# Splitting weights by two software DMAs instead of by engine subtraction, in a two-layer RWKV / attention / convolution network

## The chip, the cores and the metric

One core of a Trainium2 chip runs the whole program. The metric is device time in microseconds (us) of one execution, as the median of three runs. Engines are TensorE (PE; PEld is its weight load), VectorE (DVE), ScalarE (ACT), GpSimd (POOL) and SyncE (SP); 16 DMA engines move data.

## The reference, cut to what matters

```python
def reference(x, ...):                       # x: 1 x 1024 x 1024, float32
    for layer in range(2):
        h = rmsnorm(x, norm_mix_g[layer])
        if layer == 0:
            mix = hybrid_mixer(h, ...)       # h @ w_in, rwkv scan + window attention, @ w_out
        else:
            mix = conformer_conv(h, ...)     # h @ pw1, gate, 31-tap convolution, norm, silu, @ pw2
        x = x + mix
        h = rmsnorm(x, norm_ffn_g[layer])
        x = x + jnp.square(jax.nn.relu(h @ w1[layer])) @ w2[layer]   # 1024 -> 4096 -> 1024
    return rmsnorm(x, final_norm_g)
```

All is float32. Each of the large products (w_in, w_out, pw1, pw2, w1, w2) multiplies a weight matrix with 1024 tokens.

## The kernel before

Tokens are taken in two halves of 512; features lie on the 128 partitions. TensorE multiplies the 32-bit type fp32r, which is narrower than float32. So each operand is split into a high part (the value rounded to fp32r) and a low part (the value minus the high part), and each product is three matmuls that add up in PSUM (`mm3`, lines 299 to 301): high times high, high weights times low activations, low weights times high activations. One `mm3` is one block of 128 x 128 weights by 512 tokens.

Weights are read again for each half of the tokens. `weights` (line 273) brings them: a column block is cut into two tiles of 128 x 512 elements (256 KB), called halves below. The tile of w_in, w_out, pw1, pw2 and w1 takes four 128 x 128 blocks, in runs of 512 B in DRAM; that of w2 takes 2 x 256 columns, in runs of 1 KB. There are 720 halves: 80 of w_in, 32 of w_out, 96 of pw1 and pw2, 512 of the MLPs. For each half

- SyncE's queue loads the raw values into `wraw` (line 284),
- ScalarE casts them to fp32r in `whi` (line 286),
- VectorE or GpSimd writes `wlo = wraw - whi` (lines 288 and 271). `dve` chooses: two of three calls go to VectorE where it is None; w_in goes to VectorE where it is True; `mlp` of the stages that run beside a convolution is called with False, so there all subtractions, those of the hidden layer too (`hidl`), are on GpSimd.

`wraw`, `whi` and `wlo` have four slots each, taken in turn (`Ring`, line 1365), so a tile waits until TensorE is done with the half four before it.

The program has these stages. `run` first weaves (`weave`) the input projection, eight rwkv scans, the attention, w_out of the first half and the MLP of layer 0 for the first half into one order by hand on TensorE; this lasts about 1000 us and is called the mixer here. Then follow w_out of the second half, `conv_in(0)`, the MLP of layer 0 on the second half while VectorE does the first convolution (`conv`, line 1226: 30 multiply-adds of 128 x 512 for each of 8 channel blocks), `conv_norm`, `conv_out`, `conv_in(1)`, the MLP of layer 1 on the first half beside the second convolution, and the rest of that MLP with the last norm. Apart from the mixer on TensorE, a scheduler at build time sets the order on every engine; each engine and each DMA queue then runs its instructions strictly in that order.

Other work that the steps name: line 385 (`first_back`) reads the stored first norm `hd` back with eight transfers on GpSimd's queue; line 1183 adds an MLP product into `x`; line 1457 copies the tail of a convolution input on GpSimd; lines 617, 654 and 508 are small GpSimd steps of the scans (`BD`, `E`) and of the token shift (`carry`); lines 1157, 1158 and 1162 are relu, square and cast of the hidden layer on ScalarE.

Of the kernel before, what the change touches and what calls it, by code (L numbers as in the profile page):

```python
# [9 lines left out]
F32 = mybir.dt.float32  # L10
F32R = mybir.dt.float32r
AF = mybir.ActivationFunctionType
ALU = mybir.AluOpType
AX = mybir.AxisListType
PSUM = bass.MemoryType.PSUM
DRAM = bass.MemoryType.DRAM

P = 128
# [15 lines left out]
class Ring:  # L34
    """slots taken in turn, from one or several pools"""
# [10 lines left out]
class Net:  # L46
# [25 lines left out]
    # ---------------------------------------------------------------- order on the tensor engine  # L72
    def go(self, gen):
        """a stream on its own"""
        while True:
            try:
                next(gen)
            except StopIteration as e:
                return e.value

    def weave(self, base, *gens):
        """several streams in one order: the first of gens that is due goes on, base between them, so that the array
        stays busy; a stream yields the time (us) that its next products have to wait for the other engines, or the
        name of what has to be there"""
        due = [[0.0, g] for g in gens]
        rest = [[0.0, base]]
        share = 0.0

        def first(ds):
            return next((d for d in ds if (d[0] in self.done if isinstance(d[0], str) else d[0] <= self.clk)), None)  # L90

        while due or rest:
            f, b = first(due), first(rest)
            d = f if f and (share < LAG["SHARE"] or not b) else b
            if d is None:
                self.clk = min(d[0] for d in due + rest if not isinstance(d[0], str))
                continue
            t = self.clk
            try:
                w = next(d[1])  # L100
                d[0] = w if isinstance(w, str) else self.clk + w + (LAG["SLACK"] if w else 0.0)
            except StopIteration:
                (due if d is f else rest).remove(d)
            t = self.clk - t
            share = share + t if d is f else max(0.0, share - LAG["RATIO"] * t)

    # ---------------------------------------------------------------- constants
# [62 lines left out]
    def warm(self):  # L170
        """products that nobody reads, while the array would only wait: so its clock stays up for the first columns"""
        ps = self.mmps()
        for _ in range(4):
            self.nc.tensor.matmul(ps[:, 0:256], lhsT=self.ones, rhs=self.rst[:, 0:256], start=True, stop=True)
# [89 lines left out]
    # ---------------------------------------------------------------- helpers  # L264
    def lo(self, out, x, hi, dve=None):
        """out = x - hi, for the second part of an operand"""
        if dve is None:
            self.nlo += 1
            dve = self.nlo % 3 != 0
        eng = self.nc.vector if dve else self.nc.gpsimd  # L270
        eng.tensor_tensor(out=out, in0=x, in1=hi.bitcast(F32), op=ALU.subtract)  # L271

    def weights(self, aps, a, b, dve=None):
        """blocks of weights in two parts, k by k; loaded and split one half of them after the other"""
# [6 lines left out]
        for i in range(2):  # L281
            for ap, (his, los) in zip(aps, ws):
                raw = self.wraw.tile([P, h, b], F32, "wraw")
                nc.sync.dma_start(out=raw, in_=ap[:, i * h:(i + 1) * h, :])
                hi = self.whi.tile([P, h, b], F32R, "whi")
                nc.scalar.copy(out=hi, in_=raw)  # L286
                lo = self.wlo.tile([P, h, b], F32R, "wlo")
                self.lo(lo, raw, hi, dve)
# [33 lines left out]
    def norm_first(self, hf, rows, dst):  # L322
        """first rmsnorm by rows, then turned to feature-major; dst(u, g): where the two parts go"""
# [42 lines left out]
    def first_stored(self):  # L366
        """the second half's first norm, kept in DRAM until its place is free"""
# [20 lines left out]
    def colsum(self, xs, sq, k="n"):  # L388
        """sum over channels of x (or of its square), in two parts"""
# [29 lines left out]
    def rstd(self, accs, eps, pool, k="n"):  # L419
        """1 / sqrt(mean + eps) for every token, on every partition"""  # L420
# [56 lines left out]
    # ---------------------------------------------------------------- input projection  # L477
# [10 lines left out]
    def w_in_pair(self, js, hs):  # L488
        """two columns side by side, channel block by channel block: what is there first is used first"""
# [31 lines left out]
    # ---------------------------------------------------------------- rwkv  # L521
    def scan(self, hf, p, r, k, v, la, gl, sset, ptag, ahead):
# [86 lines left out]
        # unit lower triangular inverse: 16-blocks by substitution, then two merges  # L609
# [97 lines left out]
        # per chunk: state' = M state + C, output = R state + Y  # L707
# [114 lines left out]
    # ---------------------------------------------------------------- attention  # L822
    def attention(self, hf, i, z, qs, mi):
        """query heads 2i and 2i+1"""
# [54 lines left out]
    # ---------------------------------------------------------------- mixer of one half  # L879
# [14 lines left out]
    def shift(self, hf, j, ps, keep=False, hp=False):  # L894
        """one 128-channel column of the input projection of the rwkv part, shifted"""
# [18 lines left out]
    def twice(self, j, rows, cols, width):  # L914
        """64 channels of a column, on both halves of the partitions; cols: (from, of which half's column) pieces"""
# [6 lines left out]
    def att_in(self, hf):  # L922
        """keys with one block of the half before in front: the high part of each kv head on both halves of the
        partitions, the low parts of the first on the upper one and of the second on the lower one; values by rows"""
# [23 lines left out]
    def queries(self, hf, i, z):  # L948
        """two heads' queries, each with its high part on the half of the partitions where the low part of its keys is
        and its low part on the other one"""  # L950
# [10 lines left out]
    def att(self, hf, z):  # L961
        """attention of one half: query heads 4z to 4z+3"""
# [26 lines left out]
    def cols0(self, hs):  # L989
        """the first half's input projection"""  # L990
# [23 lines left out]
    def last1(self, h1):  # L1014
        """the last two columns, under the norm"""
# [20 lines left out]
    def scans(self, z, todo):  # L1036
        """scans one after the other in one set of tiles"""
# [39 lines left out]
    def w_out(self, hf, mi, xs, w_):  # L1077
        """output projection; the second half's input is there, the first half's comes along;
        the first half's first two columns begin with what is done, while the last scan and the attention go on"""
# [56 lines left out]
    # ---------------------------------------------------------------- mlp  # L1136
    def mlp(self, layer, halves, blocks, ahead, dve=None, close=None):
        """halves: list of (x tiles, (hi, lo)); blocks of 512 hidden channels;
        ahead: how many 128-channel pieces of a block go before the second product of the block in front;
        close: takes the second product of the last block"""  # L1140
# [57 lines left out]
    # ---------------------------------------------------------------- convolution  # L1198
# [66 lines left out]
    def row_rstd(self, ss, n):  # L1265
        """1 / sqrt(mean + eps) from n sums of squares of every row"""
# [10 lines left out]
    def final(self, hf, xs):  # L1277
        """last rmsnorm, by rows again"""
# [19 lines left out]
    def final_rows(self, hf, xs, w2, his, los):  # L1298
        """what is there so far by rows, and the second product of the last block by rows; then the last rmsnorm, one
        block of tokens after the other"""  # L1300
# [50 lines left out]
    # ---------------------------------------------------------------- the whole  # L1351
# [152 lines left out]
```

## Time and profile before

| | |
|---|---|
| median of 3 runs | 2522.08 us (2516.49, 2522.08, 2525.11) |
| span of the profiled execution | 2519.2 us, 2.9 below the median; no other time is listed for it |
| TensorE, VectorE, ScalarE, GpSimd busy | 93%, 62%, 42%, 33% |
| chain that ended last, by engine | TensorE 64%, VectorE 28%, ScalarE 3%, DMA 3% |
| mean granted TensorE clock | 0.968 |
| DMA | 236.19 MB, mean 94 GB/s; SyncE's queue 30.2% of 16 engines' span, GpSimd's 0.6% |

Busy shares are averages over stages with different limits, so they say which engines can be a bound, not where. The windows by stage and the waits say the latter. Matmuls are pipelined: one takes 389 ns in the rows, but they start 0.227 us apart, so a half (12 of them) takes 2.72 us.

### The profile page before, as it was taken

How to read it: one execution, taken by the hardware profiler on the slowest of the kernel's cores; microseconds unless marked ns; L12 is line 12 of the kernel's file. 1: busy time of each engine (PE TensorE's matmuls, PEld its weight loads, DVE VectorE, ACT ScalarE, POOL GpSimd, SP SyncE). 2: the span in 40 equal slices, each digit the busy share in tenths (PEclk: the TensorE clock that was granted, in tenths of full speed). 3: DMA queues.
4: the chain of work that ended last, by engine and by line, in shares of the span. 5: the costliest groups of instructions: out<-in, count | busy, mean ns of one | idle time of the engine just before them, and what ended most of it. 6: DMA issues, size and time to landing. Idle time of an engine off the chain costs nothing.

```text
span 2519.2 us, 38162 instructions
## 1 busy us (share of the span) xinstructions
PE 2355.4 (93%) x14525; PEld 1875.1 (74%) x14525; DVE 1568.6 (62%) x2613; ACT 1055.3 (42%) x1888; POOL 843.9 (33%) x676
## 2 busy tenths in 40 slices
PE   7999899899999999999678999997779999999998
PEld 6776677767777778777566888876657888888887
DVE  6766745647573646499998403899998025533333
ACT  6546645445352424344223543523225434433333
POOL 2223333111111112126547664226456643212221
PEclk9999999989999999999898999999889999999999
DMA  6435324313122223323112333332222332433332
GB/s 210 115 108 147 93 67 147 101 58 90 56 70 85 74 81 101 101 84 101 59 59 76 101 98 99 93 88 84 67 67 80 101 100 88 127 100 96 97 99 85
DMA packets 371851, 236.19 MB, mean 94 GB/s; under 512 B 39522, under 2 KB 355156, under 8 KB 371668
## 3 DMA queue, kind: packets, MB, share of 16 engines
q1 hardware_dynamic: 367604, 225.89, 30.2%
q0 software_dynamic: 2176, 4.19, 0.6%
q10 hardware_dynamic: 1888, 3.67, 0.4%
q8 instruction: 114, 1.87, 0.3%
q14 instruction: 69, 0.57, 0.1%
HBM read 215.35 MB, written 18.35 MB: 93 GB/s over the span
## 4 chain that ended last, share of the span: by engine, by line
PE 64%; DVE 28%; ACT 3%; DMA 3%; issue 2%; SPq 0%; POOL 0%; ACTq 0%; DVEq 0%; POOLq 0%
PE mm L299 19%; PE mm L300 18%; PE mm L301 18%; DVE acc L1226 17%; DVE x L1183 1%; DVE wlo L271 1%; DVE nt L472 1%; PE sc L603 1%; DMA raw<-p 1%; PE sc L685 1%; DVE E L662 1%; DVE C L660 1%; DVE h L271 1%; PE sc L768 1%; PE at L842 1%
## 5 line engine op out<-in xcount | busy, mean ns | idle before, releaser
L271 POOL TENSOR_TENSOR wlo<-wraw,whi 128x512 fp32r<-128x512 f32 x448 | 630.6, 1411 | 1293.6 <-ACT whi L286 1223.3
L286 ACT CAST whi<-wraw 128x512 fp32r<-128x512 f32 x720 | 445.1, 620 | 1065.8 <-PE mm L300 911.0
L299 PE MATMUL mm<-h,whi 128*128 128x512 f32 x1792 | 730.3, 408 | 10.7 <-DVE x L1183 7.1
L301 PE MATMUL mm<-h,wlo 128*128 128x512 f32 x1792 | 707.2, 395 | 7.5 <-DVE wlo L271 7.5
L300 PE MATMUL mm<-h,whi 128*128 128x512 f32 x1792 | 706.4, 394 | 0.5 <-DVE h L271 0.3
L299 PE MATMUL mm<-hidh,whi 128*128 128x512 f32 x992 | 396.0, 401 | 77.0 <-DVE x L1183 75.4
L1226 DVE SCALAR_TENSOR_TENSOR acc<-u,par,acc 128x512 f32<-128x512 f32 x480 | 466.7, 1030 | 0.1
L299 PEld LDWEIGHTS mm<-h,whi 128*128 128x128 f32 x1792 | 340.5, 190 | 93.6 <-issue 18.1
L301 PEld LDWEIGHTS mm<-h,wlo 128*128 128x128 f32 x1792 | 340.4, 190 | 85.3 <-DVE wlo L271 11.6
L301 PE MATMUL mm<-hidh,wlo 128*128 128x512 f32 x992 | 389.8, 395 | 11.2 <-POOL wlo L271 11.2
L300 PEld LDWEIGHTS mm<-h,whi 128*128 128x128 f32 x1792 | 341.3, 190 | 67.8 <-issue 2.0
L300 PE MATMUL mm<-hidl,whi 128*128 128x512 f32 x992 | 390.0, 394 | 0.3 <-DVE hidl L271 0.2
L1183 DVE TENSOR_TENSOR x<-mm,x 128x512 f32<-128x512 f32 x248 | 167.6, 685 | 291.9 <-PE mm L301 291.7
L271 DVE TENSOR_TENSOR wlo<-wraw,whi 128x512 fp32r<-128x512 f32 x272 | 194.6, 717 | 202.7 <-ACT whi L286 194.4
L299 PEld LDWEIGHTS mm<-hidh,whi 128*128 128x128 f32 x992 | 189.3, 191 | 123.1 <-issue 80.7
L301 PEld LDWEIGHTS mm<-hidh,wlo 128*128 128x128 f32 x992 | 189.1, 191 | 52.2 <-POOL wlo L271 11.6
L300 PEld LDWEIGHTS mm<-hidl,whi 128*128 128x128 f32 x992 | 189.6, 191 | 39.8 <-issue 1.1
L271 POOL TENSOR_TENSOR hidl<-rel,hidh 128x512 fp32r<-128x512 f32 x77 | 113.1, 1468 | 44.3 <-ACT hidh L1162 25.1
L1158 ACT ACTIVATE rel<-rel 128x512 f32<-128x512 f32 x128 | 80.6, 632 | 3.5
L1157 ACT ACTIVATE rel<-mm 128x512 f32<-128x512 f32 x128 | 75.5, 592 | 5.9 <-DVE u L1217 4.8
L1164 DVE CAST hidh<-rel 128x512 fp32r<-128x512 f32 x68 | 31.4, 464 | 52.5 <-ACT rel L1158 52.4
L473 ACT CAST h<-nt 128x512 fp32r<-128x512 f32 x48 | 29.7, 621 | 56.9 <-DVE nt L472 56.5
(357 smaller groups left out, 2257.3 us busy)
## 6 DMA issues: line engine op xcount, KB each, us to landing
wraw<-in_mlp_w_dram SPq DMA_DIRECT2D x512, 256.0 KB
wraw<-in_cv_pw_w_dram SPq DMA_DIRECT2D x96, 256.0 KB
wraw<-in_hy_w_in_dram SPq DMA_DIRECT2D x80, 256.0 KB
wraw<-in_hy_w_out_dram SPq DMA_DIRECT2D x32, 256.0 KB
p<-stg SPq DMA_DIRECT2D x30, 256.0 KB
raw<-p SPq DMA_DIRECT2D x40, 128.0 KB
krv<-p SPq DMA_DIRECT2D x18, 256.0 KB
xrow<-in_x_dram SPq DMA_DIRECT2D x8, 512.0 KB
```

The costliest lines, as they stand in the source:

```text
L271: eng.tensor_tensor(out=out, in0=x, in1=hi.bitcast(F32), op=ALU.subtract)
L286: nc.scalar.copy(out=hi, in_=raw)
L299: mm(ps, lhsT=whi, rhs=xhi, start=start, stop=False)
L300: mm(ps, lhsT=whi, rhs=xlo, start=False, stop=False)
L301: mm(ps, lhsT=wlo, rhs=xhi, start=False, stop=stop)
L472: nc.vector.scalar_tensor_tensor(out=t, in0=xs[c], scalar=self.pv(gname, c), in1=r, op0=ALU.mult, op1=ALU.mult)
L473: nc.scalar.copy(out=his[c], in_=t)
L1157: nc.scalar.activation(out=t, in_=ps, func=AF.Relu)
L1158: nc.scalar.activation(out=t, in_=t, func=AF.Square)
L1164: nc.vector.tensor_copy(out=hi, in_=t)
L1183: nc.vector.tensor_tensor(out=x, in0=pss[o], in1=x, op=ALU.add)
L1226: nc.vector.scalar_tensor_tensor(out=acc, in0=u[:, j:j + H], scalar=self.pv(f"dw{j}", c), in1=acc, op0=ALU.mult, op1=ALU.add)
```

## The change

Only `weights` changes in what it does; everything else in the diff takes out comments and docstrings. The raw tile goes away. A transfer on GpSimd's queue casts the weights from DRAM into `whi`; ScalarE writes `-whi` into `wlo`; a second transfer on GpSimd's queue reads the same weights again and adds them onto `wlo`. `dve` no longer plays a part for weights; `self.nlo`, which counts calls to share the other subtractions, is still counted up.

```diff
         ws = [([], []) for _ in aps]
         for i in range(2):
             for ap, (his, los) in zip(aps, ws):
-                raw = self.wraw.tile([P, h, b], F32, "wraw")
-                nc.sync.dma_start(out=raw, in_=ap[:, i * h:(i + 1) * h, :])
+                src = ap[:, i * h:(i + 1) * h, :]
                 hi = self.whi.tile([P, h, b], F32R, "whi")
-                nc.scalar.copy(out=hi, in_=raw)
+                nc.gpsimd.dma_start(out=hi, in_=src)
                 lo = self.wlo.tile([P, h, b], F32R, "wlo")
-                self.lo(lo, raw, hi, dve)
+                nc.scalar.activation(out=lo, in_=hi.bitcast(F32), func=AF.Copy, scale=-1.0)
+                nc.gpsimd.dma_start(out=lo, in_=src, accum_op=ALU.add)
                 his += [hi[:, k, :] for k in range(h)]
                 los += [lo[:, k, :] for k in range(h)]
         return ws
```

GpSimd's queue holds 348 instructions or repeated groups before and 1522 after. The first place is GpSimd in the MLP of layer 0 on the second half, beside the first convolution. Before (`rel` and `hidh` belong to the hidden layer):

```order
L271 TENSOR_TENSOR wlo_12425<-wraw_12421,whi_12423 128x512
L271 TENSOR_TENSOR wlo_12431<-wraw_12427,whi_12429 128x512
L271 TENSOR_TENSOR wlo_12469<-wraw_12465,whi_12467 128x512
L271 TENSOR_TENSOR wlo_12475<-wraw_12471,whi_12473 128x512
L271 TENSOR_TENSOR hidl_12418<-rel_12414,hidh_12417 128x512
L271 TENSOR_TENSOR wlo_12513<-wraw_12509,whi_12511 128x512
```

and after the change, at the same place:

```order
L288 DMA wlo_12134<-in_mlp_w1_dram 128x4x128
L285 DMA whi_12211<-in_mlp_w1_dram 128x4x128
L288 DMA wlo_12171<-in_mlp_w1_dram 128x4x128
L285 DMA whi_12174<-in_mlp_w1_dram 128x4x128
L288 DMA wlo_12213<-in_mlp_w1_dram 128x4x128
L285 DMA whi_12216<-in_mlp_w1_dram 128x4x128
L271 TENSOR_TENSOR hidl_12124<-rel_12120,hidh_12123 128x512
L288 DMA wlo_12176<-in_mlp_w1_dram 128x4x128
L285 DMA whi_12253<-in_mlp_w2_dram 128x2x256
```

A subtraction per half has become two DMA issues, and the casting transfer of one half (the whi of number n goes with the wlo of n + 2) stands just one issue ahead of the adding transfer of the half before it.

The second place is GpSimd in the mixer, near the start of a scan of the first half (`stg`, `sh` and `carry` are the token shift, `scar`, `st` and `BD` the scan). Before:

```order
L510 COPY sh_2850<-carry_110 128x1
L271 TENSOR_TENSOR wlo_2872<-wraw_2868,whi_2870 128x512
L271 TENSOR_TENSOR wlo_2878<-wraw_2874,whi_2876 128x512
L771 COPY scar_109<-st_2412 128x64
L758 MEMSET st_4411 128x64
L617 MEMSET BD_2618 128x8x16
L271 TENSOR_TENSOR wlo_2990<-wraw_2986,whi_2988 128x512
L515 TENSOR_TENSOR stg_2853<-stg_2853,sh_2850 128x512
```

and after the change:

```order
L510 COPY sh_2806<-carry_110 128x1
L285 DMA whi_2824<-in_hy_w_in_dram 128x4x128
L285 DMA whi_2829<-in_hy_w_in_dram 128x4x128
L771 COPY scar_109<-st_2372 128x64
L288 DMA wlo_2826<-in_hy_w_in_dram 128x4x128
L288 DMA wlo_2831<-in_hy_w_in_dram 128x4x128
L758 MEMSET st_4347 128x64
L285 DMA whi_2940<-in_hy_w_in_dram 128x4x128
L617 MEMSET BD_2574 128x8x16
L285 DMA whi_2945<-in_hy_w_in_dram 128x4x128
L515 TENSOR_TENSOR stg_2809<-stg_2809,sh_2806 128x512
L288 DMA wlo_2942<-in_hy_w_in_dram 128x4x128
```

All weight traffic now passes through this queue, between the small steps of the scans.

## Rows read from the trace of the kernel before

**Rows 1.** Page, head and part 1: busy time of each engine.
```profile
span 2519.2 us, 38162 instructions
...
PE 2355.4 (93%) x14525; PEld 1875.1 (74%) x14525; DVE 1568.6 (62%) x2613; ACT 1055.3 (42%) x1888; POOL 843.9 (33%) x676
```

**Rows 2.** Page, part 4: the chain that ended last, by line.
```profile
PE mm L299 19%; PE mm L300 18%; PE mm L301 18%; DVE acc L1226 17%; DVE x L1183 1%; DVE wlo L271 1%; DVE nt L472 1%; PE sc L603 1%; DMA raw<-p 1%; PE sc L685 1%; DVE E L662 1%; DVE C L660 1%; DVE h L271 1%; PE sc L768 1%; PE at L842 1%
```

**Rows 3.** Windows, line 301 only: PE busy (count) PEld busy (count), clock, DMA share, GB/s.
```profile
0.00:1000.00 1000.00, 352.57 (x888) 169.39 (x888) 0.97 0.35 100
1000.00:1160.00 160.00, 82.94 (x213) 39.80 (x212) 1.00 0.33 96
1160.00:1360.00 200.00, 85.69 (x212) 41.85 (x212) 0.89 0.23 69
1360.00:1620.00 260.00, 144.79 (x370) 69.81 (x370) 0.99 0.31 95
1620.00:1900.00 280.00, 127.81 (x322) 61.67 (x321) 0.91 0.25 76
1900.00:2519.00 619.00, 340.73 (x877) 164.98 (x877) 1.00 0.32 99
```

**Rows 4.** Windows, all instructions, convolution windows: PE, PEld, DVE, ACT, POOL busy, clock, DMA.
```profile
1160.00:1360.00 200.00, 154.04 (x636) 124.79 (x635) 199.93 (x215) 58.40 (x97) 120.84 (x74) 0.89 0.23 69
...
1620.00:1900.00 280.00, 227.05 (x964) 184.49 (x962) 280.00 (x315) 82.94 (x138) 125.26 (x79) 0.91 0.25 76
```

**Rows 5.** Timeline of ACT and POOL, 1445 to 1449: start, duration, instruction, idle before.
```profile
1445.49 0.62 ACT L286 CAST whi<-wraw 128x512 fp32r<-128x512 f32 x1 [2.10 <-PE mm L300]
1448.21 0.62 ACT L286 CAST whi<-wraw 128x512 fp32r<-128x512 f32 x1 [2.10 <-PE mm L300]
...
1446.19 1.29 POOL L271 TENSOR_TENSOR wlo<-wraw,whi 128x512 fp32r<-128x512 f32 x1 [1.43 <-ACT whi L286]
```

**Rows 6.** Waits, whole run: who waited for whom, us in total, times, longest.
```profile
ACT whi L286 <- PE mm L300: 911.0, 470, 29.0
...
POOL u L1457 <- DVE acc L1226: 56.1, 7, 23.1
...
POOL E L654 <- PE sc L628: 35.8, 6, 16.2
...
POOL BD L617 <- DVE ar L573: 25.8, 2, 14.5
POOL carry L508 <- ACT sh L504: 25.6, 5, 16.0
```

**Rows 7.** Page, part 5: the two groups of weight subtractions, GpSimd's and VectorE's.
```profile
L271 POOL TENSOR_TENSOR wlo<-wraw,whi 128x512 fp32r<-128x512 f32 x448 | 630.6, 1411 | 1293.6 <-ACT whi L286 1223.3
...
L271 DVE TENSOR_TENSOR wlo<-wraw,whi 128x512 fp32r<-128x512 f32 x272 | 194.6, 717 | 202.7 <-ACT whi L286 194.4
```

**Rows 8.** Line 385, GpSimd's only DMA issues: ns min/median/max, and landing.
```profile
L385 POOL DMA_DIRECT2D h<-hd x8: 713/714/901, 187.7 to 211.5; - x8
...
DMA to landing us min/median/max: 4.0/4.4/5.6
```

**Rows 9.** DMA queues, 186 to 218, GpSimd's queue: packets, MB, share of engines.
```profile
q0 software_dynamic: 2176, 4.19, 47.9%
```

**Rows 10.** DMA queues and issues, 1400 to 1500: SyncE's queue and its loads.
```profile
q1 hardware_dynamic: 15200, 9.96, 32.7%
...
wraw<-in_mlp_w_dram SPq DMA_DIRECT2D x39, 256.0 KB
```

**Rows 11.** The chain in order of time, a piece that is a transfer: start, us.
```profile
124.43 2.46 DMA d<-E
```

**Rows 12.** Groups, DVE line 1226: 1160 to 1360, 1620 to 1900, 1317 to 1328.
```profile
L1226 DVE SCALAR_TENSOR_TENSOR acc<-u,par,acc 128x512 f32<-128x512 f32 x183 | 182.2, 1058 | 0.0
...
L1226 DVE SCALAR_TENSOR_TENSOR acc<-u,par,acc 128x512 f32<-128x512 f32 x240 | 236.6, 1045 | 0.0
...
L1226 DVE SCALAR_TENSOR_TENSOR acc<-u,par,acc 128x512 f32<-128x512 f32 x16 | 10.8, 741 | 0.0
```

## The prediction

> **What bounds the kernel now.** I read the page's busy times first, then the chain of waits, then windows by stage, then the waits, and last the DMA rows. [rows 1] show TensorE busy for 2355.4 of 2519.2 us; [rows 2] show the chain on the three split products (lines 299 to 301, 55% together) and, for 17%, on VectorE's convolution (line 1226). A "half" below is 256 KB of weights: four blocks, four triples of products, so four instructions of line 301. [rows 3] then give the halves of each stage, as count over four, and there are three stages. The **mixer** (0 to 1000) uses 888/4 = 222 halves, one per 4.5 us. The two **convolution windows** (1160 to 1360 and 1620 to 1900) use (212+322)/4 = 133.5 halves in 480 us, 3.6 us each; there VectorE is busy without a gap while TensorE works 154.0 of 200 and 227.1 of 280 us [rows 4], so it stands idle for 99 us. The **rest** (160 + 260 + 619 = 1039 us) uses (213+370+877)/4 = 365 halves at 2.85 us.
>
> In the rest TensorE sets the pace: two casts of line 286 follow each other in 2.72 us, and each waited for TensorE, not for data [rows 5]. Over the run ScalarE's cast waited 911.0 us for TensorE to give a slot back [rows 6]: weights are ready ahead, and the split is hidden. So the change can gain only where VectorE or GpSimd hold something up, which is the convolution, and can lose wherever a half takes longer than its stage allows.
>
> **The change part by part.** It removes 448 subtractions from GpSimd (630.6 us) and 272 from VectorE (194.6 us) [rows 7], and 720 loads from SyncE's queue, which nobody waited for in the rest. ScalarE has 720 negations for 720 casts of the same tile, 0.62 us each, so its sum stays; what changes is that a negation waits for a transfer just issued, where the cast found its data loaded. It adds 1440 issues to GpSimd's queue, in order, and the adding transfer waits there for the negation.
>
> *Issue time g.* The only GpSimd issues of before take 0.71 us [rows 8], for 256 runs of 2 KB; a half of w1 has 512 runs of 512 B, one of w2 256 of 1 KB. So 0.71 if it is a fixed price, 1.43 if it goes by runs; I take 1.0 for the casting and 1.1 for the adding transfer, nearer to the fixed price because half of the tiles have 256 runs.
>
> *Casting transfer, issue to landing, Lh.* Those eight 512 KB loads land in 4.0 to 5.6, median 4.4 us [rows 8]. They took 47.9% of 32 us of all 16 engines, 1.92 us each [rows 9]; a half took 32.7% of 100 us over 39, 0.84 us [rows 10]. So 4.4 − 1.92 + 0.84 = 3.3; with 0.4 for more runs 3.7. Bounds: 2.46, a 128 KB transfer of the hardware queue [rows 11], and 5.6.
>
> *Adding transfer, Ll.* No row shows one. It reads its destination besides its source. I take 3.7 + 0.84 for the second stream + 0.4 for descriptors, 4.9. Bounds: 2.46, as if it were plain, and 5.6 + 0.84 + 0.72 = 7.2.
>
> *Pace of a half, T.* A hop between engines is 0.08, say 0.1 us (1445.49 + 0.62 to 1446.19) [rows 5]; the negation is 0.62 and I add 0.3, half of one cast, for standing behind other ScalarE work. GpSimd's order is casting n+1, adding n, casting n+2. Three loops follow.
> (a) Adding n−1 is issued (1.1), casting n+1 lands (3.7), hop, negation, hop, adding n+1: 1.1 + 3.7 + 0.1 + 0.92 + 0.1 = 5.92 per two halves, 2.96.
> (b) Four slots: TensorE frees a slot, hop, casting (3.7), hop, negation (0.92), hop, adding (4.9), hop, TensorE until the half is done (2.72, less 0.45 as wlo is first needed by the third product): 12.2 per four, 3.05.
> (c) Casting n+1 waits for half n−3, and adding n stands behind it: 0.1 + 1.0 + 4.9 + 0.1 + 2.27 = 8.37 per three, 2.79.
> All lie near one another, and landings scatter by 1.6 us, so the pace is a little over the slowest: I take **T = 3.2**, between 2.72 (TensorE's own) and 4.1 (loop b with 5.6 and 7.2: 16.4/4; loop a: 8.15/2 = 4.1).
>
> *Sum.* Rest: 365 × (3.2 − 2.72) = +175. Convolution: 133.5 × 3.2 = 427 for 480, so −53. This needs VectorE to be done in 427 too: its 183 and 240 instructions of line 1226 last 1.06 and 1.05 us there, beside GpSimd's subtractions, and 0.74 in a stretch where GpSimd does little but wait and copy 30 columns [rows 12]. 423 × 0.31 = 131 us less, so it fits. Mixer: 3.2 is under 4.5, so the mean is covered. But GpSimd's queue now carries weights, and what waits at its head holds them up: the waits for E, BD and carry, 35.8 + 25.8 + 25.6 = 87 us [rows 6], formerly on an engine with nothing urgent behind. I take them whole, +87; the bounds are 0 and about 250, if ScalarE's scan work also stands behind negations that wait. Startup, where the first halves arrive some 5 us later, I cost at nothing: TensorE waits for the first norm then. Sum: 2519.2 + 175 − 53 + 87 = 2728. The runs' median is 2522.1, 2.9 above this execution, so **2730 us**.
>
> The Trainium skill, page "SBUF — State Buffer", section "Who interferes with whom", says that a VectorE instruction with two SBUF inputs contends with a GpSimd instruction that reads SBUF, not with one that only writes. By it descriptor work leaves line 1226 alone, as the sum has it; if issues hindered it as subtractions do, the −53 would fall away and 2783 would come out. Line 1226 at 1.05 against 0.74 us bears out its first half; no run here shows the second.
>
> **The rivals.**
> *A, latencies are short (faster).* Once Lh + Ll is below 7.3, loop b is under 2.72 and supply is hidden again. The convolution windows then shrink to TensorE's 381 us, −99, and the mixer costs 0 to 87: 2423 to 2510, middle 2463. For it: hardware-queue transfers of 2.46 us, and that the loads of 4.4 us were twice as large. Against: even the quickest GpSimd load took 4.0 us, and the adding transfer moves more. Whole-run break-even is at 499T = 365 × 2.72 + 480 − 87, T = 2.78.
> The skill's page "DMA: Bandwidth & Descriptors", section "Anatomy of one DMA — SWDGE (gpsimd) path", gives 2.0 us plus bytes/436e3; an estimate from it is 2.6 us for a half, and rival A would be right. For 512 KB it gives 3.2 where the trace has 4.0 to 5.6, so the trace disagrees and I give A little.
> *B, the DMA engines become the bound.* A half has 0.84 us for the casting transfer; at T = 3.2 the adding one may take 2.36, 2.8 plain prices. Above that the engines decide. At four plain prices T = 0.84 + 3.36 = 4.2: rest 365 × 1.48 = +540, convolution 133.5 × 4.2 − 480 = +81, mixer 87 and as much again for bursts, +174: 2522 + 795 = 3317. For it: runs of 512 B, and read, add and write in one pass, with no row for the price. Against: two plain streams are only 1.68 us, and all weights hold only 32.7% of the engines there now [rows 10].
> *C, near break-even*, Lh + Ll at 7.3 to 7.9: 2500 to 2560.
> That the transfers copy without rounding, so that the low part is empty, is possible; bytes and waits would be the same, and so would the time. GpSimd's copies of line 1457, which waited 56.1 us for the convolution [rows 6], hold up weights in both kernels and change no case.
>
> **How the numbers follow.** The forecast (T from 2.85 to 3.7, 2560 to 3000 us) has 0.55: all three loops, which use the nearest rows, lie above 2.72, and every surprise but one adds to them. B has 0.20 (3000 to 3600), A 0.15, C 0.10. About 0.3%, 7.5 us, is what can be told from no change; of C 0.02 is faster, 0.04 within, 0.04 slower. So faster 0.17, same 0.04, slower 0.79. The range leaves out the better half of A and the worst third of B: 2460 to 3400; 3400 is also what the upper bounds give (T = 4.1: 2522 + 504 + 67 + 250 = 3343).
>
> **What would show it.** In the profile after, TensorE must wait for the adding transfer of wlo, in the rest above all, where the line-301 rate falls from one half per 2.85 to about 3.3 us; line 1226 must come near 0.74 us and the convolution windows must shrink; GpSimd's issues should last 0.7 to 1.4 us and land in 3.5 to 5; ScalarE's waits should move from TensorE to the DMA of whi. If the rest keeps 2.8 us per half, A is right. If the DMA engines are busy above 90% there, B is. If the loss lies mostly before 1000 us, the queue order in the mixer was underrated.

## The result and the profile after

The changed kernel takes **3029.78 us** (median of 4 runs, 3018.89 to 3043.8) against 2519.28 us for the kernel before on the same chip: ratio **1.2031**, interval 1.1989 to 1.2072. The forecast was 2730: the direction was right and the time lies in the range (2460 to 3400), but the loss is 510 us where 208 was forecast. The profiled execution spans 3041.8 us, 522.6 above that of before; the working below goes by it.

The page of the changed kernel: head, busy times (part 1), the GpSimd queue's row of part 3, and the chain by engine and by line (part 4).

```profile
span 3041.8 us, 38386 instructions
...
PE 2546.6 (84%) x14525; PEld 1885.9 (62%) x14525; DVE 1219.5 (40%) x2341; ACT 1055.7 (35%) x1885; POOL 1696.9 (56%) x1668
...
q0 software_dynamic: 629376, 381.77, 79.3%
...
issue 29%; POOL 27%; DMA 19%; PE 17%; ACT 4%; DVE 2%; POOLq 0%; ACTq 0%; SPq 0%; DVEq 0%
POOL whi L285 14%; POOL wlo L288 11%; DMA whi<-in_mlp_w_dram 7%; DMA wlo<-in_mlp_w_dram 4%; PE mm L301 4%; PE mm L299 4%; PE mm L300 3%; DMA whi<-in_hy_w_in_dram 2%; POOL hidl L271 1%; ACT wlo L287 1%; DMA whi<-in_cv_pw_w_dram 1%; DMA wlo<-in_cv_pw_w_dram 1%; DMA raw<-p 1%; DMA wlo<-in_hy_w_in_dram 1%; PE sc L685 1%
```

TensorE's share of the span fell from 93% to 84% [rows 1], and the chain, which ran through the products and VectorE's convolution [rows 2], now runs through GpSimd's issues (27%), their landings (19%) and time for which the profile shows no wait ("issue", 29%). As the next views show, the kernel waits for a loop.

Where the time went: windows of the changed kernel, line 301 only, cut near the counts of [rows 3] (columns as there).

```profile
0.00:1170.00 1170.00, 370.14 (x888) 175.65 (x889) 0.93 0.78 135
1170.00:1376.00 206.00, 91.26 (x213) 42.23 (x214) 0.95 0.93 143
1376.00:1601.00 225.00, 87.05 (x212) 41.34 (x211) 0.90 0.76 123
1601.00:1934.00 333.00, 148.99 (x371) 68.75 (x370) 0.98 0.91 146
1934.00:2250.00 316.00, 133.96 (x323) 61.82 (x322) 0.94 0.87 137
2250.00:3041.00 791.00, 349.68 (x876) 163.69 (x875) 0.98 0.90 150
```

Row by row against [rows 3]: the mixer +170; the rest +46, +73 and +173 (791.8 for 619.2), together +292; the convolution windows +25 and +36, +61. The sum is 523. Forecast were +87, +175 and -53. In the kernel before, TensorE has a wait of 7 us (1358 to 1365) and one of 5 us (1898.5 to 1903.5) across the cuts at 1360 and 1900; with every run cut at exactly the same product, some 10 us move from the convolution windows to the rest (+51 and +302 here). That holds for every run below alike.

The loop itself: timeline of GpSimd and ScalarE in the last stage (start, duration, instruction, idle before and what ended it).

```profile
2708.56 1.29 POOL L288 DMA_DIRECT2D wlo<-in_mlp_w_dram  x1 [2.90 <-ACT wlo L287]
2709.33 1.28 POOL L285 DMA_DIRECT2D whi<-in_mlp_w_dram  x1
2710.91 1.28 POOL L288 DMA_DIRECT2D wlo<-in_mlp_w_dram  x1 [0.30 <-ACT wlo L287]
2711.85 1.11 POOL L285 DMA_DIRECT2D whi<-in_mlp_w_dram  x1
2715.65 1.28 POOL L288 DMA_DIRECT2D wlo<-in_mlp_w_dram  x1 [2.69 <-ACT wlo L287]
...
2714.41 0.63 ACT L287 ACTIVATE wlo<-whi 128x512 fp32r<-128x512 f32 x1 [3.79 <-DMA whi<-in_mlp_w_dram]
2716.84 0.63 ACT L287 ACTIVATE wlo<-whi 128x512 fp32r<-128x512 f32 x1 [1.80 <-DMA whi<-in_mlp_w_dram]
```

This is the prediction's loop (a), with other numbers. Adding n-1 starts at 2708.56; casting n+1 can start 0.77 behind it (2709.33); it lands and its negation starts 5.08 later (2714.41); the negation takes 0.63; adding n+1 starts 0.61 behind it (2715.65). 0.77 + 5.08 + 0.63 + 0.61 = 7.09 us for two halves, **3.55 each**. GpSimd stands idle for 2.69 to 2.90 us in each turn, ScalarE for longer, and in this turn no slot is waited for. In the median of the last stage the four steps are 0.77, 5.01, 0.63 and 0.30, 6.7 us; the turn shown is a slow one by its last step. Over 2700 to 2900 line 301 has 228 instructions, 57 halves, 3.51 us each.

Waits of the changed kernel, whole run (who waited for whom, us, times, longest).

```profile
ACT wlo L287 <- DMA whi<-in_mlp_w_dram: 1141.2, 413, 28.2
POOL wlo L288 <- ACT wlo L287: 909.4, 468, 6.4
...
PE mm L301 <- DMA wlo<-in_mlp_w_dram: 286.9, 246, 25.8
...
POOL whi L285 <- PE mm L301: 185.6, 117, 10.4
```

Before, ScalarE waited 911.0 us for TensorE to give slots back [rows 6]; now it waits for data, and TensorE for the adding transfer. Page, part 6, the landings of the changed kernel (KB, median us from issue to landing):

```profile
whi<-in_mlp_w_dram POOLq DMA_DIRECT2D x512, 256.0 KB, 4.8
wlo<-in_mlp_w_dram POOLq DMA_DIRECT2D x512, 256.0 KB, 4.6
```

### The profile page after: what moved, and what is told of

The parts are those of the page before. It is cut to its first block, busy times and chain, and to the rows that moved or that the text cites. A ratio compares the mean times of both kernels' runs of the same rounds, so it can differ in the third digit from the quotient of the medians.

```text
span 3041.8 us, 38386 instructions
## 1 busy us (share of the span) xinstructions
PE 2546.6 (84%) x14525; PEld 1885.9 (62%) x14525; DVE 1219.5 (40%) x2341; ACT 1055.7 (35%) x1885; POOL 1696.9 (56%) x1668
## 3 DMA queue, kind: packets, MB, share of 16 engines
q0 software_dynamic: 629376, 381.77, 79.3%
## 4 chain that ended last, share of the span: by engine, by line
issue 29%; POOL 27%; DMA 19%; PE 17%; ACT 4%; DVE 2%; POOLq 0%; ACTq 0%; SPq 0%; DVEq 0%
POOL whi L285 14%; POOL wlo L288 11%; DMA whi<-in_mlp_w_dram 7%; DMA wlo<-in_mlp_w_dram 4%; PE mm L301 4%; PE mm L299 4%; PE mm L300 3%; DMA whi<-in_hy_w_in_dram 2%; POOL hidl L271 1%; ACT wlo L287 1%; DMA whi<-in_cv_pw_w_dram 1%; DMA wlo<-in_cv_pw_w_dram 1%; DMA raw<-p 1%; DMA wlo<-in_hy_w_in_dram 1%; PE sc L685 1%
## 5 line engine op out<-in xcount | busy, mean ns | idle before, releaser
L287 ACT ACTIVATE wlo<-whi 128x512 fp32r<-128x512 f32 x720 | 454.2, 631 | 1689.9 <-DMA whi<-in_mlp_w_dram 1141.2
L288 POOL DMA_DIRECT2D wlo<-in_mlp_w_dram x512 | 657.1, 1294 | 646.1 <-ACT wlo L287 592.1
L301 PE MATMUL mm<-h,wlo 128*128 128x512 f32 x1792 | 756.9, 423 | 264.7 <-DMA wlo<-in_mlp_w_dram 176.4
L299 PE MATMUL mm<-h,whi 128*128 128x512 f32 x1792 | 748.7, 418 | 14.6 <-ACT stg L514 7.9
L300 PE MATMUL mm<-h,whi 128*128 128x512 f32 x1792 | 722.7, 403 | 0.0
L285 POOL DMA_DIRECT2D whi<-in_mlp_w_dram x512 | 563.1, 1106 | 165.3 <-PE mm L301 127.2
L1226 DVE SCALAR_TENSOR_TENSOR acc<-u,par,acc 128x512 f32<-128x512 f32 x480 | 343.3, 781 | 0.3
L288 POOL DMA_DIRECT2D wlo<-in_cv_pw_w_dram x96 | 127.0, 1323 | 136.3 <-ACT wlo L287 124.0
L271 POOL TENSOR_TENSOR hidl<-rel,hidh 128x512 fp32r<-128x512 f32 x77 | 182.7, 2373 | 23.1 <-ACT hidh L1162 13.7
L288 POOL DMA_DIRECT2D wlo<-in_hy_w_in_dram x80 | 106.6, 1374 | 154.8 <-ACT wlo L287 131.6
L285 POOL DMA_DIRECT2D whi<-in_hy_w_in_dram x80 | 81.5, 1034 | 75.5 <-PE mm L301 46.3
```

The costliest lines, as they stand in the source:

```text
L285: nc.gpsimd.dma_start(out=hi, in_=src)
L287: nc.scalar.activation(out=lo, in_=hi.bitcast(F32), func=AF.Copy, scale=-1.0)
L288: nc.gpsimd.dma_start(out=lo, in_=src, accum_op=ALU.add)
L299: mm(ps, lhsT=whi, rhs=xhi, start=start, stop=False)
L300: mm(ps, lhsT=whi, rhs=xlo, start=False, stop=False)
L301: mm(ps, lhsT=wlo, rhs=xhi, start=False, stop=stop)
```

## The experiments

Two theories were set against each other. **L**: the pace is latency divided by the halves that GpSimd's order keeps on the way; the order (adding n straight behind casting n+1) allows two. **D**: the DMA engines' own time per half is the bound. The rows of queue q0 price it, in packet time averaged over the 16 engines: 79.3% of 3041.8 us is 2412 us, 3.35 per half; the DMA share of the last stage is 0.90.

| run | time, us | ratio to before, interval | rest / convolution / mixer against the span of before |
|---|---|---|---|
| the change itself | 3029.8 | 1.2031 (1.1989 to 1.2072) | +292 / +61 / +170 |
| 1: no adding transfer | 2440.7 | 0.9691 (0.9655 to 0.9726) | -9 / -62 / -9 |
| 2: second transfer plain | 2634.5 | 1.046 (1.0421 to 1.05) | +60 / -8 / +63 |
| 3: six slots each | 2876.0 | 1.1419 (1.1376 to 1.1462) | +195 / +17 / +145 |
| 4: load and cast as before | 2547.0 | 1.0111 (1.0082 to 1.014) | +21 / -34 / +38 |
| 5: seven and five slots | 2451.5 | 0.9738 (0.9697 to 0.9778) | -1 / -84 / +30 |
| 6: the same, second plain | 2436.3 | 0.9676 (0.9662 to 0.9691) | -11 / -75 / +1 |
| 7: five and three slots | 2732.3 | 1.0841 (1.0812 to 1.0871) | +84 / +9 / +118 |
| 8: four and two slots | 3656.1 | 1.4509 (1.4451 to 1.4567) | +558 / +177 / +418 |
| 9: adding beside convolution only | 2470.9 | 0.981 (0.9775 to 0.9846) | +6 / -44 / -1 |
| 10: before's split in the mixer, then seven and five | 2432.2 | 0.9654 (0.9622 to 0.9685) | +1 / -85 / -2 |
| 11: the change, hidl on VectorE | 2942.4 | 1.1722 (1.1644 to 1.18) | +267 / -12 / +162 |
| 12: run 10, hidl on VectorE | 2410.4 | 0.9574 (0.9542 to 0.9607) | +2 / -106 / -4 |

The last column is worked out from windows of each trace, cut near the counts of [rows 3] as above for the change. Runs 1, 2 and 6 leave out the addition that makes the low part of the weights, so only their times count.

**1. No adding transfer.**

```diff
-                nc.gpsimd.dma_start(out=lo, in_=src, accum_op=ALU.add)
```

> The adding transfer is left out: the low part of the weights is only the negative of the high part. Two theories of the changed kernel's 3.5 us per half in its last stages. Theory L (latency): GpSimd's queue holds casting n+2 behind adding n+1, which waits for the negation of a casting transfer that takes 4.9 us to land whatever else runs, so 1.3 + 4.9 + 0.63 + hops make 6.9 us per two halves. Theory D (DMA engines): the engines are 93% busy there, the landing is long because adding transfers are in its way, and the pace is their service time. Without the adding transfer both expect a kernel that no longer waits for weights, 2440 to 2540 us, since the order on the queue no longer holds a chain. What differs is the casting transfer: L expects it to land in 4.5 to 5.0 us still, with GpSimd's queue at 25 to 40% of the DMA engines; D expects 3.0 to 3.8 us, and that the queue's share falls by two thirds or more.

Measured 2440.7, in the range that both theories gave.

**2. The second transfer overwrites.**

```diff
-                nc.gpsimd.dma_start(out=lo, in_=src, accum_op=ALU.add)
+                nc.gpsimd.dma_start(out=lo, in_=src)
```

> The second transfer overwrites instead of adding, so the low part of the weights is the weight itself; order, waits and bytes read from DRAM are those of the changed kernel. L expects the same chain: 2950 to 3050 us, landings of 4.5 to 5 us for both transfers. D expects the engines' load to fall by the second read: share in the last stages from 93% to 70% or less, landings under 4.2 us, pace 3.0 us or less per half, 2700 to 2850 us in all.

Measured 2634.5, under both ranges. The landings, page part 6, first without an adding transfer, then with a plain second one:

```profile
whi<-in_mlp_w_dram POOLq DMA_DIRECT2D x512, 256.0 KB, 3.2
```

```profile
whi<-in_mlp_w_dram POOLq DMA_DIRECT2D x512, 256.0 KB, 3.5
wlo<-in_mlp_w_dram POOLq DMA_DIRECT2D x512, 256.0 KB, 3.4
```

A casting transfer alone lands in 3.2 us, beside plain ones in 3.5, beside adding ones in 4.8. So L was wrong to take the landing as fixed "whatever else runs": the adding transfer is dear, and dear to its neighbour. Its own engine time comes from queue q0's rows (run 1, run 2, run 4 below, page part 3):

```profile
q0 software_dynamic: 315776, 192.98, 39.1%
...
q0 software_dynamic: 629376, 381.77, 72.4%
...
q0 software_dynamic: 315776, 192.98, 57.4%
```

The queue has 39.1% of 2439.3 us in run 1, 1.32 per half; in run 4 below (only adding transfers) 57.4% of 2544.6, **2.03**; in run 2 72.4% of 2634.6, 2.65 for two plain ones. The prices add up (1.32 + 2.03 = 3.35). The landings pointed to D; but at a shorter landing loop (a) is shorter too (0.77 + 3.5 + 0.63 + 0.6 = 5.5, 2.75 per half), so they don't separate the two.

**3. Six slots for whi and wlo each.**

```diff
-        wslots = {n: [(wp, n + str(i)) for i in range(4)] for n in ("wraw", "whi", "wlo")}
+        wslots = {n: [(wp, n + str(i)) for i in range(6)] for n in ("wraw", "whi", "wlo")}
```

> Six slots each for the high and the low part of the weights instead of four. In most places the order on GpSimd's queue still has one casting transfer ahead of the adding one. L expects little, since the chain through the queue's order does not depend on slots: 2900 to 3040 us, with gains only where two casting transfers now go ahead. D expects no change: 3000 to 3050 us. Below 2850 us both are wrong and the slots (loop b of the prediction) were the bound.

Measured 2876.0, under both ranges. The windows of this run, line 301 (columns as above), say why:

```profile
1600.00:1700.00 100.00, 52.91 (x140) 26.16 (x140) 1.00 1.11 182
2500.00:2800.00 300.00, 147.14 (x354) 67.22 (x353) 0.98 0.94 155
```

In most stretches the order is the change's, and 354/4 halves take 300 us, 3.39 each, two slots more or not: loop (a) has no slot in it. In some (128 of the 498 halves behind the mixer) casting n+2 stands ahead of adding n. In the upper row, where it does so for 21 of 34 halves (in the lower for none of 89), a half takes 100/35 = 2.86 us, **under D's 3.35, at a DMA share of 1.11**. A share above 1 means that packet times overlap on an engine; 0.9 is not full.

**4. Load and cast as before, adding transfer kept** (wraw, SyncE's load and ScalarE's cast come back).

```diff
+                raw = self.wraw.tile([P, h, b], F32, "wraw")
+                nc.sync.dma_start(out=raw, in_=src)
                 hi = self.whi.tile([P, h, b], F32R, "whi")
-                nc.gpsimd.dma_start(out=hi, in_=src)
+                nc.scalar.copy(out=hi, in_=raw)
```

> One half of the change alone: the raw weights come by SyncE's queue and ScalarE casts them, as before; ScalarE then writes the negative and the adding transfer on GpSimd's queue makes the low part. L expects supply to be hidden again, since nothing on GpSimd's queue waits for a transfer just issued and four slots of 0.1 + 0.63 + 0.1 + 4.7 + 0.1 + 2.27 us are 2.0 us per half: the last stages at 2.75 to 2.85 us per half, line 1226 at 0.75 us, 2440 to 2540 us in all. D expects the adding transfer to hold the engines for over 2 us beside 0.84 for the plain load: 2.9 to 3.1 us per half in the last stages and 2580 to 2750 us in all.

Measured 2547.0, between the two ranges and in neither, so it does not separate them: the adding transfers still land in 5.1 us (median, MLP weights), but no adding transfer stands before a casting one in the queue.

**5. Seven slots for whi, five for wlo.** The same twelve slots as in run 3, the same transfers and bytes. A negation now waits for its own slot too, and by then the next casting transfer is out: the order is casting n+2, adding n in 475 of the 498 halves behind the mixer.

**6. The same with a plain second transfer.** The slots of both:

```diff
-        wslots = {n: [(wp, n + str(i)) for i in range(4)] for n in ("wraw", "whi", "wlo")}
+        wslots = {n: [(wp, n + str(i)) for i in range(m)] for n, m in (("wraw", 1), ("whi", 7), ("wlo", 5))}
```

> All transfers of the change stay; whi gets seven slots and wlo five (twelve together, as in the run with six of each), so that a negation waits for its own slot and GpSimd's order becomes casting n+2, adding n, casting n+3, adding n+1 in 475 of the 498 halves behind the mixer. Theory L (the loop through GpSimd's order): the same 7.1 us loop (adding issue 1.27, casting landing 4.8, negation 0.63, hops) now spans three halves, 2.4 us each, so TensorE's 2.72 to 2.85 sets the pace: rest +0 to +50, convolution -60 to -99, mixer about +140 as with six of each: 2560 to 2660. Theory D (the DMA engines' own time, 1.33 us for a casting and 2.03 for an adding transfer, 3.35 per half): pace stays at 3.35 and the time stays where six slots of each left it, 2840 to 2900.

> As the run with seven and five slots, but the second transfer overwrites instead of adding (the low part is then the weight itself): the price of adding is gone, the order stays. Theory L: rest +0, convolution -60 to -99, mixer +58 as in the run with plain second transfers and four slots: 2470 to 2520. Theory D: two plain transfers take 2.65 us of the engines, just under TensorE's pace: 2480 to 2560, near the other. If it stays at 2630, it is neither order nor adding but the second stream itself.

Measured 2451.5 and 2436.3, both below the ranges given for L, which had put too much on the mixer. The whole change, adding transfers and all, is now 2.6% **faster** than the kernel before, and the price of adding is hidden but for 15 us. D is out. Page of run 5, queue row and landings, and its windows of line 301:

```profile
q0 software_dynamic: 629376, 381.77, 97.1%
...
whi<-in_mlp_w_dram POOLq DMA_DIRECT2D x512, 256.0 KB, 4.7
wlo<-in_mlp_w_dram POOLq DMA_DIRECT2D x512, 256.0 KB, 5.0
```

```profile
0.00:1030.00 1030.00, 355.55 (x889) 170.90 (x889) 0.97 0.89 154
1030.00:1188.00 158.00, 84.12 (x213) 39.96 (x212) 0.99 1.24 188
1188.00:1342.00 154.00, 82.01 (x214) 40.37 (x213) 0.99 1.10 179
1342.00:1597.00 255.00, 141.20 (x371) 69.38 (x370) 1.00 1.19 193
1597.00:1839.00 242.00, 127.16 (x322) 61.84 (x321) 0.96 1.10 175
1839.00:2464.00 625.00, 338.75 (x876) 164.34 (x875) 0.99 1.12 188
```

Landings are as long as in the changed kernel (4.7 and 5.0 for 4.8 and 4.6). The rest stands at the pace of before; behind the mixer the DMA shares are 1.10 to 1.24, where the change had 0.76 to 0.93. The expectation had left the mixer at +140; it went to +30 as well, and in run 6 to +1. Timeline of GpSimd and ScalarE of the same run:

```profile
2210.42 0.74 POOL L285 DMA_DIRECT2D whi<-in_mlp_w_dram  x1
2211.31 1.19 POOL L288 DMA_DIRECT2D wlo<-in_mlp_w_dram  x1
2213.14 0.74 POOL L285 DMA_DIRECT2D whi<-in_mlp_w_dram  x1 [0.65 <-PE mm L301]
...
2204.94 0.63 ACT L287 ACTIVATE wlo<-whi 128x512 fp32r<-128x512 f32 x1 [1.08 <-PE mm L301]
2210.38 0.63 ACT L287 ACTIVATE wlo<-whi 128x512 fp32r<-128x512 f32 x1 [1.02 <-PE mm L301]
```

GpSimd and ScalarE wait for TensorE again: 2204.94 to 2210.38 is 5.44 us for two halves, TensorE's 2.72.

**7. Five and three slots; 8. four and two.** The order of run 5 with eight slots, as many as the change has, and with six.

> Eight slots, as many as the change has, but five for whi and three for wlo: the order on GpSimd's queue is that of seven and five (casting n+2 ahead of adding n in 487 of 498 halves behind the mixer). If the order is the cause (theory L): loop (a) over three halves 2.4 us; wlo's three slots give hop 0.1 + negation 0.93 + hop 0.1 + landing 5.0 + hop 0.1 + products 2.27 = 8.5 per three, 2.83; whi's five 13.4/5 = 2.7. So some 2.85 to 3.0 per half against 2.75: 2480 to 2600. If it was the number of slots: at or above the change's 3030.

> Four slots for whi and two for wlo: again casting n+2 ahead of adding n (496 of 498), but now wlo's loop is the longest, 8.5 us per two halves, 4.25: rest 365 x 1.5 = +550, convolution 133.5 x 4.25 - 480 = +87, mixer +50 to +150: 3200 to 3300. If the order alone decided, and slots were worth nothing: as with five and three, 2480 to 2600.

Measured 2732.3 and 3656.1, both above their ranges. At the change's eight slots the order alone takes back 297 of the 578 us between 3029.8 and 2451.5; the four slots more take the rest. In the late stage the slot loops were about right: 265/4 halves in 2300 to 2500 of run 7 are 3.02 us each (2.83 expected), 364/4 in 3000 to 3400 of run 8 4.40 (4.25). The miss is elsewhere. The convolution windows are +9 and +177, where the expected paces give about -100 to -80 and +87: in run 7 two subtractions of hidl on GpSimd, of the kind that run 11 takes up, last 29.64 and 29.92 us there, and TensorE's longest wait for wlo in the first window is 28.5 us. The mixer is +118 and +418, where +50 to +150 was expected of run 8: there TensorE does scan work between the products of a half, so a slot may come back later than the loops have it. That last step is argued, not shown.

**9. Adding transfers beside the convolution only** (elsewhere the split of before; there load, cast, negation, adding transfer). **10. Before's split in the mixer, the change's behind it,** with seven and five slots (the raw tile's four are handed on). Of both edits only the switches are shown, of run 9 the first of two; `weights` chooses by `self.mode`.

```diff
+        self.mode = "add"
         self.go(self.mlp(0, [(x1, self.norm(x1, "nf0", 1))], range(8), 2, False))
+        self.mode = "sub"
```

```diff
+        self.mode = "dma"
+        self.whi.slots = self.whi.slots + self.wraw.slots[:3]
+        self.wlo.slots = self.wlo.slots + self.wraw.slots[3:]
         x0, mi1, hslots = self.x0, self.mi[1], self.hslots
```

> Split of the kernel before everywhere, but in the two products that run beside the convolution: there load by SyncE and cast by ScalarE as before, then the negation by ScalarE and the adding transfer. If relief of VectorE beside the convolution is what the adding transfer is worth, and the 25 us that the same split cost over the whole kernel were lost in the mixer (its trace is 38 us behind there, and makes up some 40 us in the two convolution windows): 2465 to 2495. If the loss came with the adding transfer everywhere: 2515 to 2550.

> Split of the kernel before in the mixer (loads, casts, subtractions); behind it the split of the change, with seven slots for whi and five for wlo (the four slots of the raw weights are given to them). Theory L: mixer +0, rest +0 to +50, convolution -60 to -99: 2440 to 2510. Theory D: rest 365 halves at 3.35 instead of 2.72 to 2.85, +190 to +230, convolution -30: 2670 to 2720.

Measured 2470.9, in the first range, and 2432.2, 8 us below theory L's range for run 10 and far from D's. What the change has to give lies in the convolution windows (-85), and with this order the change costs nothing in the rest (+1).

**11. The change with hidl on VectorE beside the convolution.** After run 5 one loss of the change was still without a cause: in the convolution windows a half takes 541/133.5 = 4.05 us, though loop (a) gives 3.5 and line 1226 is as fast as forecast. Timeline of GpSimd and of VectorE in the changed kernel:

```profile
1377.24 1.27 POOL L288 DMA_DIRECT2D wlo<-in_mlp_w_dram  x1 [0.77 <-ACT wlo L287]
1378.00 1.29 POOL L285 DMA_DIRECT2D whi<-in_mlp_w_dram  x1
1378.83 27.72 POOL L271 TENSOR_TENSOR hidl<-rel,hidh 128x512 fp32r<-128x512 f32 x1
1406.51 1.27 POOL L288 DMA_DIRECT2D wlo<-in_mlp_w_dram  x1
...
1369.56 35.87 DVE L1226 SCALAR_TENSOR_TENSOR acc<-u,par,acc 128x512 f32<-128x512 f32 x54
```

One subtraction of hidl, of which the median takes 1.70 us in this trace, is on record with 27.72. VectorE runs 54 convolution steps in a row, 0.66 us each, to 1405.43; the subtraction ends at 1406.55, and the weights' issues stand behind it.

```diff
-                    self.lo(lo, t, hi, dve)
+                    self.lo(lo, t, hi, True if dve is False else dve)
```

> The change with its four slots and its order; only the hidden layer's low part (hidl, 56 or so subtractions beside the two convolutions) goes to VectorE instead of GpSimd. In the change's trace four of these on GpSimd last 27.7, 6.5, 19.4 and 10.2 us where the others last 1.3 to 1.8; each stands across a row of convolution steps on VectorE, and weight transfers wait behind it (TensorE's longest waits there are 25.8 and 17.9 us). If GpSimd's subtraction is held off by VectorE's steps: these waits go, the convolution windows shrink by 30 to 60 us, 2970 to 3000. If it was another wait that these records hide, or the subtraction is as late in VectorE's queue: 3015 to 3060.

Measured 2942.4, 87 us under the change and better than the range. Waits of TensorE and convolution windows (line 301) of this run:

```profile
PE mm L301 <- DMA wlo<-in_mlp_w_dram: 205.5, 224, 4.7
```

```profile
1364.00:1548.00 184.00, 84.25 (x214) 39.55 (x213) 0.99 0.95 153
...
1872.00:2156.00 284.00, 129.38 (x322) 60.27 (x323) 0.99 0.96 152
```

TensorE's longest wait fell from 25.8 to 4.7 us and the windows from 541 to 468, which is 133.5 x 3.5: the pace of the rest.

**12. Run 10 with hidl on VectorE:**

> The split of the kernel before in the mixer and that of the change with seven and five slots behind it, as in the run of that name, and hidl on VectorE beside the convolution. There TensorE waits only 15.5 us for wlo in the first convolution window and not at all in the second, and VectorE is busy 148.0 of 168 and 222.4 of 227 us. If the held-off subtraction still costs there: 15 to 20 us less, 2410 to 2420. If VectorE is the bound there, its 56 more subtractions of 0.7 us are 39 us on it, partly in its 24 idle us: 2430 to 2455.

Measured **2410.4**, 4.3% under the kernel before and the best of all; the interval (0.9542 to 0.9607) lies below that of run 10.

## Why the prediction was right in sign and wrong in size

The mechanism of the pace was right and a size in it was not: the casting transfer's landing was put at 3.7 us and took 4.8 to 5.0. Two more terms failed: the convolution's -53, and the mixer's +87.

*What bounds before.* Right: supply is hidden there, and the runs show what the convolution can give: -62 when nothing follows the casting transfer (run 1), -106 with adding transfers and hidl off GpSimd (run 12).

*Issue time g.* 1.0 and 1.1 were taken. Records of both kinds last some 1.28 us in the turn shown (0.74 in run 2, without adding), but the next issue starts 0.77 us behind an adding one, so on the path 0.77 counts: an overestimate of 0.3.

*Casting transfer Lh: the term that failed.* 3.7 was taken from loads that stood alone. Alone it is 3.2 and beside a plain second transfer 3.5, so the estimate was good for that; beside adding transfers it is 4.8 (5.08, with the hop to ScalarE, in the turn shown). The working put the price of adding into Ll alone, and Ll came out near what was said (4.9 taken, 4.6 measured), but the working did not have that it slows the casting transfer next to it. How much depends on how close they run: with fewer slots and a slower pace casting ones land in 4.0 (run 7) and 3.3 us (run 8).

*Pace T.* The order was read rightly and loop (a) is the one that binds, though the working had loop (b) ahead of it, 3.05 to 2.96. With the terms of the turn shown it is 7.09 per two halves, 3.5 instead of 2.96 per half; besides the landing, the hop to the adding issue was too short (0.1 taken, 0.61 there and 0.30 in the median), which issue time and negation, both put too high, make up for. T = 3.2 became 3.51: 365 x 0.31 = 113 of the 117 us by which the rest exceeds +175. Loops (b) and (c) wait for slots, and in the late stage (2250 to 3041) GpSimd waited 26 us for slots and 273 us for negations.

*Convolution.* The -53 became +61 in two parts. At 3.5 a half the windows take 467, not 427 (run 11: 468), and another 73 went when hidl left GpSimd (run 11), where its subtractions had lasted up to 27.72 us across VectorE's steps. The forecast relied on VectorE being released, and it was: line 1226 went from 1.05 [rows 12] to 0.781 us on average (page, part 5, of the changed kernel):

```profile
L1226 DVE SCALAR_TENSOR_TENSOR acc<-u,par,acc 128x512 f32<-128x512 f32 x480 | 343.3, 781 | 0.3
```

What it missed is that the GpSimd subtraction left over stands in the weights' own queue. The trace of before had a sign of it, in the very stretch of [rows 12] in which VectorE's steps last 0.74 us: GpSimd's copy of 30 columns is on record with 6.57 us, where the other seven last 0.21 to 3.32, their median 0.67 (timeline of GpSimd, before).

```profile
1321.45 6.57 POOL L1457 COPY u<-u 128x30 f32<-128x30 f32 x1 [6.51 <-DVE acc L1226]
```

The Trainium skill, "SBUF — State Buffer", section "Who interferes with whom", has a two-input VectorE instruction contend with a GpSimd instruction that reads SBUF, not with one that only writes it; the prediction counted descriptor work as the latter, and the trace agrees (0.781).

*Mixer.* +87 became +170, and by another mechanism. GpSimd's waits for E, BD and carry, 87 us before [rows 6], are down to 2 us (groups of GpSimd, 0 to 1170, the changed kernel):

```profile
L654 POOL COPY E<-e 64x256 f32<-64x256 f32 x8 | 6.5, 811 | 0.2 <-PE sc L628 0.2
L617 POOL MEMSET BD<- 128x128 f32 x8 | 5.1, 637 | 0.0
L508 POOL COPY carry<-sh 128x1 f32<-128x1 f32 x6 | 1.9, 319 | 2.0 <-ACT sh L504 2.0
```

Those small steps no longer waited at the queue's head; the weights were themselves late. In 0 to 1160 ScalarE's negations waited 435 us for landings (259.0 + 138.0 + 37.9 in three rows), with scan work behind them, and TensorE 73.6 us for wlo. The bound of 250 had named scan work behind negations; the 170 lie within it. With seven and five slots the mixer costs 30, and with plain second transfers in the same queue 1 (run 6). Part of the 170 goes with the clock: at a mean granted clock of 0.93, where it was 0.97 [rows 3], the same matmuls keep TensorE busy for 1015.5 us (0 to 1170) instead of 954.0 (0 to 1000), 61 us more; no run holds the clock apart. How the rest divides between late negations and late wlo was not tried.

*Rival A* needed Lh + Ll under 7.3: run 2 has 6.9, and takes 2634, not 2463 (the middle of its 2423 to 2510 would be 2466). The sum of latencies alone did not decide; the order did (run 6, landings of 3.4 and 3.6, 2436). The estimate of 2.6 us for a half from the Trainium skill ("DMA: Bandwidth & Descriptors", section "Anatomy of one DMA — SWDGE (gpsimd) path"), which spoke for A, is below the 3.2 measured alone; giving it little was right. *Rival B* would have been confirmed by the text's own sign, DMA engines above 90% in the rest (0.90 to 0.93 there). The sign was wrong: the same transfers went through at 1.24.

Of the other signs listed, the line-301 rate in the rest went to one half per 3.65 us, past the 3.3 named; TensorE's waits for wlo, ScalarE's move from TensorE to the landing of whi, line 1226, issues of 0.7 to 1.4 and landings of 3.5 to 5 came as said; the convolution windows did not shrink, and the loss does not lie mostly before 1000 us.

Two slips of the working decide nothing: its upper bounds give 3343, not 3400, and only the 256 tiles of w2, of 720, have 256 runs, which is not half.

## What to carry to other kernels

Where two dependent transfers of a tile go through one in-order queue, work out how many tiles the queue's order keeps on the way, and divide the loop's latency by it; two slots more of each brought only 3.39 for 3.51 us per half where most of the order stayed (run 3), and giving the first tile two slots more than the second changed it here. Price a transfer beside the ones it will run with, not alone, and do not read a DMA share near 1 as a full engine. After moving work off an engine, look at what little is left on it: it may now stand in the way of something urgent.

## What the hardware showed that was not expected

- An adding transfer of 256 KB takes 2.03 us of packet time on each of the 16 DMA engines (run 4), a casting one 1.32 (run 1), and beside adding ones, in place of plain ones, a casting one lands in 4.8 instead of 3.5 us (the change, run 2).
- The DMA share of a stretch reached 1.24 (run 5), so packet times overlap on an engine.
- A GpSimd subtraction of hidl (median 1.70 us) was on record with 27.72 us across a row of 54 VectorE steps (others with 19.37 and 10.18), where in the kernel before the longest of 77 took 1.846, with convolution steps of 1.05 us. Moving it to VectorE took the waits away (run 11); what holds it off inside the chip was not shown. In the section "Who interferes with whom" of the Trainium skill's "SBUF — State Buffer", whoever issues first has the shared ports for its whole instruction, said there of VectorE's two-port modes; one convolution step is 0.66 us here, and the trace shows a wait over some 40 of them.
